# A hybrid layer on one Trainium2 core: stick-breaking v as a fifth seven-product pair, a longer weave, and T1 sums by accumulating loads

## The chip, the core and the metric

The kernel runs on one core of one Trainium2 chip. The core has TensorE (PE, matrix multiplication, 128 x 128), VectorE (DVE), ScalarE (ACT), GpSimd (POOL) and SyncE (SP), a working memory of 128 partitions (SBUF) and eight banks of accumulator memory (PSUM, 512 float32 per partition in each). Every engine takes its instructions in the order in which they were issued to it; SP and POOL also issue DMAs, which all run on the core's 16 DMA engines. The metric is device time in microseconds for one execution, the median of several runs.

## The reference

One layer over 256 tokens of width 2048, all in float32: an FFN (SwiGLU, width 5632), a mixer with two parallel branches, a second FFN, a small embedding gate, with a layer norm after each of the first three. The change concerns the mixer:

```python
proj = x @ w_in
mq, mk, mv, mo, mi, mf, sq, sk, sv, ga, gb = _split_cols(proj)
qk = jax.nn.silu(_causal_conv(jnp.concatenate([mq, mk], axis=-1), conv_w))
...
h = _mlstm_chunkwise(q, k, mv, log_i, log_f)          # 4 heads of 256
h = _head_norm(h, norm_g)
y_m = h * jax.nn.sigmoid(mo)
y_sb = _stick_breaking(sq, sk, sv)                    # 8 heads of 128
merged = jax.nn.sigmoid(ga) * (y_m @ w_up_m) + jax.nn.sigmoid(gb) * (y_sb @ w_up_sb)
return merged @ w_out
```

`w_in` has 11272 columns: q, k, v and output gate of the mLSTM (1024 each), eight gate columns, stick-breaking q, k and v (1024 each), and the two branch gates ga and gb (2048 each).

## The kernel before

**Weights and units.** A weight tile is 256 rows by 512 columns of a weight matrix (512 KB). It is loaded into a page ("raw", one of 48 pages of 4 KB per partition), and then split into two float32r parts: ScalarE casts the high part (line 1213), VectorE subtracts to get the low part (line 1217). A *unit* of the program is six matmuls (lines 1264 to 1266, twice): one weight tile against one token tile of 128, high by high, high by low and low by high. A plain *group* of 512 output columns has eight weight tiles, each used by two units (both token tiles), so 16 units.

**Pairs of seven products.** `seven` and `both7` compute two column groups at once with seven products in the manner of Strassen-Winograd, where the two token tiles and the two groups are the halves. For each of the four chunks of 512 rows there are the products 1 and 2 (of plain weights), and 5, 7, 6, 4, 3, whose weights are sums of raw tiles and whose activations are sums too ("forms", made by `form_turn`). A pair has 28 units, each with a weight of its own, so 28 splits. Product 1 and 2 go first; the five others are interleaved chunk by chunk, so that five PSUM banks are held until the last chunk. The first sum, T1, is b11 + b12. With `loaded` false VectorE makes it (`plus`, line 361); with `loaded` true the raw tile b12 is loaded, and b11 is added by an accumulating DMA from GpSimd's queue (line 1190), and in the last chunk the third sum is made so too. The FFNs' pairs are loaded.

**Order.** A planner walks the program unit by unit and issues the instructions of all engines in the final order. It keeps a clock of its own (`sched.now`, 6 x 0.2161 for a unit) and a heap of small tasks with due times (`DELAY`), which it runs after each unit; `bank` and `spaced` push tasks that need a PSUM bank at least `BANK_GAP` apart. Splits are issued until the number in hand reaches a limit, and raw tiles are loaded up to a limit as well (`HELD`: raw tiles and splits for each mode, set by `Mode` marks in the program). All PSUM tiles, products and small ones alike, share eight banks.

**The mixer.** Its program is, in this order: six plain groups (q of heads 0 and 1; the gates with stick-breaking q of heads 0 and 1; the other q and k groups), then the mLSTM tasks are spawned, then two groups for the mLSTM's v; then the forms of x1T are spawned (`forms_later`); then two plain groups, stick-breaking v of heads 0 to 3 and k and q of heads 0, 1, 2, 3; then `sticks` spawns the eight heads of stick-breaking; and then the *weave*. `weave(main, side)` deals the units of the side list evenly between the units of the main list. Main has 144 units: stick-breaking projections (the second half of v among them), the two gates of column group 0 (`branch`), and the up-projections of groups 0, 1, 2 (`ups`). Side has four pairs, 112 units: the mLSTM's output gate, and the pairs of gates of column groups 1, 2 and 3. After the weave come the up-projections of group 3 and the output projection.

**Tasks.** `mlstm(h)` goes through five PSUM tiles: the decay matrix (line 857), scores (867), numerator with denominator for each token tile (881). VectorE reads the denominator from PSUM three times in small operations (882 to 885), and ScalarE then scales the numerator out of PSUM. `gated(h)` waits for the output gate, multiplies, transposes into PSUM (916) and splits the result into ymT, which is put away to DRAM by `put_ym_away` and brought back by `bring_ym_back`, before the up-projections use it. `stick(h)` needs q, k and v of its head (lines 935 to 965); heads start `STICK_GAP` apart.

Each column of the window tables below is one engine; the DMA share is that of the 16 DMA engines.

Of the kernel before, what the change touches and what calls it, by code (L numbers as in the profile page):

```python
# [13 lines left out]
P = 128  # L14
# [15 lines left out]
HELD = {"ffn": (8, 6), "mix": (5, 6), "wide": (8, 6)}  # L30
# [16 lines left out]
STICK_GAP = 14.0  # L47
# [138 lines left out]
def kernel(  # L186
# [30 lines left out]
    def bank(delay):  # L217
        return sched.slot(delay, BANK_GAP)
# [469 lines left out]
    def sb_columns(ps, t, heads):  # L688

        n = len(heads) * DS  # L690
        if heads[0] >= 16:
            if ("sv", t) not in st:
                st["sv", t] = big()
            c0 = (heads[0] - 16) * DS
            nc.scalar.copy(st["sv", t][:, c0:c0 + n], ps[:, :n])
            flags.update(("sv", t, h - 16) for h in heads)
        else:
            stage = temp()
            nc.scalar.copy(stage[:, :n], ps[:, :n])
            sched.spaced(sb_turn(t, stage, heads), DELAY["sbt"], BANK_GAP)  # L700
# [152 lines left out]
    def mlstm(h):  # L853
        yield from wait("gates", ("qk", 0, h), ("qk", 1, h), ("v", 0, h // 2), ("v", 1, h // 2))
        d = temp()
# [5 lines left out]
        yield DELAY["m0"]  # L861
# [9 lines left out]
        yield DELAY["m1"]  # L871
        mv = small.tile([P, TT, 2], F32, name="hmv", tag="hmv")
        r = small.tile([P, TT], F32, name="hr", tag="hr")
        if ("hs", h // 2) not in st:
            st["hs", h // 2] = big().rearrange("q (g t e) -> q g t e", g=2, t=TT)
        hs = st["hs", h // 2][:, h % 2]
        for t in range(TT):
            ps = misc([P, DM + 1])
            for s in range(t + 1):
                off = s * 256 + (t - s) * P  # L880
                nc.tensor.matmul(ps[:], d[:, off:off + P], st["v", s, h // 2][:, h % 2], start=(s == 0), stop=(s == t))  # L881
            nc.vector.tensor_scalar(out=r[:, t:t + 1], in0=ps[:, DM:], scalar1=-1.0, scalar2=st["em"][:, t, h:h + 1],
                                    op0=ALU.mult, op1=ALU.max)
            nc.vector.tensor_tensor(out=r[:, t:t + 1], in0=ps[:, DM:], in1=r[:, t:t + 1], op=ALU.max)
            nc.vector.reciprocal(out=r[:, t:t + 1], in_=r[:, t:t + 1])
            yield DELAY["m2"]
            activate(hs[:, t], ps[:, 0:DM], ACT.Copy, scale=r[:, t:t + 1])
# [15 lines left out]
    def gated(h):  # L903
# [6 lines left out]
        for t in range(TT):  # L910
            nc.vector.tensor_tensor(out=hs[:, t], in0=hs[:, t], in1=st["mo", t][:, h * DM:(h + 1) * DM], op=ALU.mult)
        for t in range(TT):
            yield bank(0.0 if t else DELAY["m4"])
            ps = misc([P, 2, P])
            for b in range(2):
                nc.tensor.transpose(ps[:, b], hs[:, t, b * P:(b + 1) * P], ident[:])
            dst = ymT.get(h // 2, t)
            parts = [(dst[:, :, 2 * (h % 2) + b], ps[:, b], st["cw"][:, 64 + 2 * h + b:65 + 2 * h + b]) for b in range(2)]
            for d, src, g in parts:
                activate(d[:, 0], src, ACT.Copy, scale=g)  # L920
            for d, src, g in parts:
                nc.vector.scalar_tensor_tensor(out=d[:, 1], in0=src, scalar=g, in1=d[:, 0], op0=ALU.mult, op1=ALU.subtract)
# [54 lines left out]
    for which, g in ((0, 1), (1, 0), (1, 1)):  # L977
        program.extend(flat(group(w_in, range(0, D, 2 * P), which * 1024 + g * COL, COL, x1T, qk_done(which, g))))
    program.append(lambda: [sched.spawn(in_sequence([mlstm(a), mlstm(a + 1)])) for a in (0, 2)])
    for g in range(2):  # L980
        program.extend(flat(group(w_in, range(0, D, 2 * P), 2048 + g * COL, COL, x1T, v_done(g))))
    program.append(lambda: [sched.spawn(forms_later(x1T, c), 6.0 + 14.0 * c) for c in range(4)])

    def sb(*heads):
        if heads[0] >= 16:
            col0 = sq0 + heads[0] * DS
        else:
            col0 = [(sq0 + h * DS, 2 * DS) for h in heads[::2]]
# [3 lines left out]
    program.extend(sb(16, 17, 18, 19))  # L992
    program.extend(sb(8, 9, 2, 3))
# [308 lines left out]
```

## Time and profile before

| | us |
|---|---|
| median of 3 runs | 2188.23 |
| lowest, highest | 2187.34, 2188.68 |
| the profiled execution, its own time | 2186.12 |
| its span (first to last instruction) | 2184.4 |
| end of the mLSTM's v groups, in the span | 855.38 |
| start of the weave | 908.72 |
| start of the last up-projections | 1272.77 |

The profile is of one execution. Its page has the busy time of each engine, the DMA queues, the chain of work that ended last, and groups of instructions by line; further views of the same trace give the busy time in any window, the waits, and the instructions in order of time. A row of a group reads: line, engine, operation, output<-inputs, shapes, count | busy us, mean ns of one | idle time just before them and who ended it. A row of the timeline reads: start, length, engine, line, operation. q1 is the hardware queue that SP feeds, q0 the software queue that GpSimd feeds. Granted TensorE clock was 1.00 in the whole span.

### The profile page before, as it was taken

The page shows a single profiled execution, that of the slowest core. Times are in us where ns is not written, and L with a number is a line of the kernel's source. Part 1 is how long each engine was busy: PE and PEld are TensorE (multiplying, and loading weights), DVE is VectorE, ACT ScalarE, POOL GpSimd, SP SyncE. Part 2 cuts the span into 40 slices and gives each one's busy share as a digit, 9 for nine tenths or more (in the row PEclk, how much of TensorE's full clock was granted, in tenths as well). Part 3 has the DMA queues.
Part 4 walks back from the last instruction along what each step waited for, and adds up shares of the span by engine and source line. Part 5 has one row for each costly group of instructions (what it writes and reads, how often), then busy time and mean ns, then how long its engine had stood idle before and what let it go on. Part 6 is the DMA issues. An engine that isn't in the chain of part 4 may idle for free.

```text
span 2184.4 us, 28262 instructions
## 1 busy us (share of the span) xinstructions
PE 2174.9 (100%) x9966; PEld 1800.5 (82%) x9966; DVE 1903.3 (87%) x2108; ACT 1316.2 (60%) x1591; POOL 97.9 (4%) x88
## 2 busy tenths in 40 slices
PE   9999999999999999999999999999999999999999
PEld 7888888888888888888888888888888888888888
DVE  6899999999998865898988985799999999999974
ACT  7565655556664754667775554566665556665572
POOL 0100000010000000000000000000010000000000
PEclk9999999999999999999999999999999999999999
DMA  9899999999994775667878886589999999999753
GB/s 332 252 302 284 289 293 308 281 277 315 310 331 158 219 229 154 193 210 207 301 216 282 268 270 212 181 237 310 286 278 305 297 283 291 312 299 316 254 165 103
DMA packets 302223, 568.52 MB, mean 260 GB/s; under 512 B 18265, under 2 KB 39681, under 8 KB 302081
## 3 DMA queue, kind: packets, MB, share of 16 engines
q1 hardware_dynamic: 280320, 524.77, 72.0%
q0 software_dynamic: 21760, 41.95, 11.2%
q8 instruction: 78, 1.28, 0.2%
q14 instruction: 65, 0.52, 0.1%
HBM read 560.35 MB, written 6.29 MB: 259 GB/s over the span
## 4 chain that ended last, share of the span: by engine, by line
PE 98%; DVE 1%; ACT 0%; issue 0%; DMA 0%; SPq 0%; DVEq 0%; ACTq 0%
PE mm L1264 31%; PE mm L1266 31%; PE mm L1265 31%; PE ms L290 1%; DVE split L1217 1%; PE ms L495 0%; ACT split L1213 0%; PE ms L959 0%; PE ms L867 0%; PE ms L881 0%; PE ms L935 0%; PE ms L948 0%; DMA big<-in_x_dram 0%; PE ms L705 0%; DVE raw L361 0%
## 5 line engine op out<-in xcount | busy, mean ns | idle before, releaser
L1213 ACT CAST split<-raw 128x1024 fp32r<-128x1024 f32 (+2 forms) x1061 | 1060.7, 1037 | 514.2 <-PE mm L1265 144.4
L1217 DVE TENSOR_TENSOR split<-raw,split 128x1024 fp32r<-128x1024 f32 (+2 forms) x1061 | 1242.9, 1203 | 129.8 <-ACT split L1213 113.9
L1264 PE MATMUL mm<-split,actT 128*128 128x512 f32 (+2 forms) x3120 | 1216.7, 390 | 0.1
L1266 PE MATMUL mm<-split,actT 128*128 128x512 f32 (+2 forms) x3120 | 1203.0, 386 | 1.7 <-DVE actT L297 1.7
L1265 PE MATMUL mm<-split,actT 128*128 128x512 f32 (+2 forms) x3120 | 1201.7, 385 | 0.0
L1266 PEld LDWEIGHTS mm<-split,actT 128*128 128x128 f32 x3120 | 586.0, 188 | 122.7 <-DVE actT L297 3.4
L1265 PEld LDWEIGHTS mm<-split,actT 128*128 128x128 f32 x3120 | 586.9, 188 | 114.1 <-DVE split L1217 2.0
L1264 PEld LDWEIGHTS mm<-split,actT 128*128 128x128 f32 x3120 | 586.6, 188 | 114.3 <-issue 1.3
L361 DVE TENSOR_TENSOR raw<-raw 128x1024 f32<-128x1024 f32 x240 | 293.0, 1221 | 2.2
L1190 POOL DMA_DIRECT2D raw<-in_ffn_w_dram x80 | 95.4, 1193 | 1877.5 <-DVE temp L559 774.1
L292 ACT CAST actT<-ms 128x512 fp32r<-128x512 f32 x60 | 35.1, 587 | 86.5 <-PE ms L290 84.7
L568 DVE TENSOR_TENSOR temp<-mm,temp 128x512 f32<-128x512 f32 x112 | 77.0, 687 | 3.5 <-PE mm L1266 1.3
L621 DVE SCALAR_TENSOR_TENSOR big<-mm,big 128x512 f32<-128x512 f32 x96 | 65.6, 685 | 4.8 <-PE mm L1266 4.8
L297 DVE TENSOR_TENSOR actT<-ms,actT 128x512 fp32r<-128x512 f32 x60 | 40.9, 687 | 19.4 <-ACT big L296 10.6
L236 ACT ACT_TABLE_LOAD x35 | 44.9, 1283 | 0.6
L285 DVE TENSOR_TENSOR actT<-temp,actT 128x512 fp32r<-128x512 f32 x40 | 26.5, 689 | 17.3 <-ACT actT L284 17.2
L240 ACT ACTIVATE temp<-mm 128x512 f32<-128x512 f32 (+1 forms) x22 | 12.2, 559 | 43.6 <-PE mm L1266 43.5
L240 ACT ACTIVATE temp<-temp 128x512 f32<-128x512 f32 (+1 forms) x48 | 28.6, 595 | 9.2 <-DVE temp L568 6.6
L284 ACT CAST actT<-temp 128x512 fp32r<-128x512 f32 x40 | 24.1, 620 | 13.1 <-DVE temp L308 12.2
L794 DVE SCALAR_TENSOR_TENSOR temp<-ms,cw,temp 128x253 f32<-128x253 f32 (+2 forms) x48 | 22.4, 480 | 7.3 <-ACT temp L240 6.1
L1076 DVE SCALAR_TENSOR_TENSOR big<-big,mm 128x512 f32<-128x512 f32 x8 | 5.5, 686 | 25.3 <-PE mm L1266 25.3
L240 ACT ACTIVATE temp<-ms,gbT 128x128 f32<-128x128 f32 x64 | 24.1, 460 | 5.5 <-PE ms L495 5.5
(128 smaller groups left out, 539.5 us busy)
## 6 DMA issues: line engine op xcount, KB each, us to landing
raw<-in_ffn_w_dram SPq DMA_DIRECT2D x655, 512.0 KB, 6.2
raw<-in_w_in_dram SPq DMA_DIRECT2D x176, 512.0 KB, 4.4
raw<-in_ffn_w_dram POOLq DMA_DIRECT2D x80, 512.0 KB, 8.9
raw<-in_w_out_dram SPq DMA_DIRECT2D x32, 512.0 KB, 6.4
raw<-in_w_in_dram SPq DMA_DIRECT2D x56, 256.0 KB, 3.6
raw<-in_w_ple_gate_dram SPq DMA_DIRECT2D x24, 512.0 KB, 6.0
raw<-in_w_up_sb_dram SPq DMA_DIRECT2D x16, 512.0 KB, 5.1
raw<-in_w_up_m_dram SPq DMA_DIRECT2D x16, 512.0 KB, 5.5
```

Source lines behind the costliest of these rows:

```text
L236: nc.scalar.preload_act_table_set(table[0])
L240: nc.scalar.activation(out, in_, func, **kw)
L297: nc.vector.tensor_tensor(out=dst[:, 1], in0=ps[:], in1=dst[:, 0], op=ALU.subtract)
L361: nc.vector.tensor_tensor(out=out.tile[:, :, :cols], in0=a.tile[:, :, :cols], in1=b.tile[:, :, :cols], op=ALU.add)
L568: nc.vector.tensor_tensor(out=out, in0=a, in1=b, op=op)
L621: nc.vector.scalar_tensor_tensor(out=xs, in0=ps, scalar=0.5, in1=xs, op0=ALU.mult, op1=ALU.add)
L1190: nc.gpsimd.dma_start(out=r.tile[:, :, :r.cols], in_=r.plus[0], accum_op=ALU.add)
L1213: nc.scalar.copy(hi[:, ks], r[:, ks])
L1217: nc.vector.tensor_tensor(out=lo[:, ks], in0=r[:, ks], in1=hi[:, ks], op=ALU.subtract)
L1264: nc.tensor.matmul(ps, hi, w[0][:, k, :u.cols], start=first, stop=False)
L1265: nc.tensor.matmul(ps, hi, w[1][:, k, :u.cols], start=False, stop=False)
L1266: nc.tensor.matmul(ps, lo, w[0][:, k, :u.cols], start=False, stop=last)
```

## The change

- Stick-breaking v (1024 columns) leaves the main list and the plain groups, and becomes a fifth pair of seven products, first in the side list, with T1 made by VectorE. `sv_dest` and `sv_ready` place its four results and set the flags for which the sticks wait.
- The weave begins where the two plain groups were: main still has 144 units (the k and q group of heads 0, 1, 2, 3 is now its first), side has 140. In its first part a new mode, "woven", holds six raw tiles instead of eight; the mode "wide" begins after two main groups.
- The four other pairs are made with `loaded` true.
- The forms of x1T are spawned after the second group of mLSTM q, 16 instead of 14 apart.
- `mlstm` asks for its PSUM tiles through `bank`. ScalarE copies numerator and denominator out of PSUM for each token tile, VectorE works on the denominators of both tiles from SBUF (four small operations a head instead of six), and ScalarE scales in SBUF.
- `gated` transposes both token tiles into one PSUM bank.
- `bring_ym_back` is issued half a group earlier, and the up-projections of group 0 use ymT first instead of ysbT. `STICK_GAP` is 13 instead of 14.

```diff
-HELD = {"ffn": (8, 6), "mix": (5, 6), "wide": (8, 6)}
+HELD = {"ffn": (8, 6), "mix": (5, 6), "woven": (6, 6), "wide": (8, 6)}
...
-STICK_GAP = 14.0
+STICK_GAP = 13.0
...
+    def sv_dest(k, t):
+        if ("sv", t) not in st:
+            st["sv", t] = big()
+        return st["sv", t][:, k * COL:(k + 1) * COL]
+
+    def sv_ready(k, t):
+        flags.update(("sv", t, 4 * k + h) for h in range(4))
...
     def mlstm(h):
         yield from wait("gates", ("qk", 0, h), ("qk", 1, h), ("v", 0, h // 2), ("v", 1, h // 2))
+        yield bank(0.0)
...
-        yield DELAY["m0"]
+        yield bank(DELAY["m0"])
...
-        yield DELAY["m1"]
+        yield bank(DELAY["m1"])
...
-            nc.vector.tensor_scalar(out=r[:, t:t + 1], in0=ps[:, DM:], scalar1=-1.0, scalar2=st["em"][:, t, h:h + 1],
-                                    op0=ALU.mult, op1=ALU.max)
-            nc.vector.tensor_tensor(out=r[:, t:t + 1], in0=ps[:, DM:], in1=r[:, t:t + 1], op=ALU.max)
-            nc.vector.reciprocal(out=r[:, t:t + 1], in_=r[:, t:t + 1])
-            yield DELAY["m2"]
-            activate(hs[:, t], ps[:, 0:DM], ACT.Copy, scale=r[:, t:t + 1])
+            nc.scalar.copy(hs[:, t], ps[:, 0:DM])
+            nc.scalar.copy(den[:, t:t + 1], ps[:, DM:])
+            yield DELAY["m2"] if t else bank(DELAY["m2"])
+        nc.vector.tensor_scalar(out=r[:], in0=den[:], scalar1=-1.0, scalar2=None, op0=ALU.mult)
+        nc.vector.tensor_tensor(out=r[:], in0=den[:], in1=r[:], op=ALU.max)
+        nc.vector.tensor_tensor(out=r[:], in0=r[:], in1=st["em"][:, :, h], op=ALU.max)
+        nc.vector.reciprocal(out=r[:], in_=r[:])
+        yield DELAY["m2"]
+        for t in range(TT):
+            activate(hs[:, t], hs[:, t], ACT.Copy, scale=r[:, t:t + 1])
+        yield DELAY["m2"]
...
+        yield bank(DELAY["m4"])
+        ps = misc([P, TT, 2, P])
+        parts = []
         for t in range(TT):
-            yield bank(0.0 if t else DELAY["m4"])
-            ps = misc([P, 2, P])
...
+        if which == 0:
+            program.append(lambda: [sched.spawn(forms_later(x1T, c), 6.0 + 16.0 * c) for c in range(4)])
     program.append(lambda: [sched.spawn(in_sequence([mlstm(a), mlstm(a + 1)])) for a in (0, 2)])
     for g in range(2):
         program.extend(flat(group(w_in, range(0, D, 2 * P), 2048 + g * COL, COL, x1T, v_done(g))))
-    program.append(lambda: [sched.spawn(forms_later(x1T, c), 6.0 + 14.0 * c) for c in range(4)])
...
-    program.extend(sb(16, 17, 18, 19))
-    program.extend(sb(8, 9, 2, 3))
...
     def pair(g):
-        return both7(w_in, ga0 + g * COL, ga0 + D + g * COL, x1T, gate_dest(g), gate_ready(g), False)
+        return both7(w_in, ga0 + g * COL, ga0 + D + g * COL, x1T, gate_dest(g), gate_ready(g), True)

     program.append(sticks)
-    main = sb(10, 11, 4, 5) + sb(20, 21, 22, 23) + sb(12, 13, 6, 7) + sb(14, 15) + branch(0, 0) + branch(0, 1) + [bring_ym_back] + ups(0, True) + ups(1) + ups(2)
-    mode("wide")
-    program.extend(weave(main, both7(w_in, 3072, 3072 + COL, x1T, mo_dest, mo_ready, False) + pair(1) + pair(2) + pair(3)))
+    gate = branch(0, 1)
+    main = sb(8, 9, 2, 3) + sb(10, 11, 4, 5) + [Mode("wide")] + sb(12, 13, 6, 7) + sb(14, 15) + branch(0, 0) + gate[:8] + [bring_ym_back] + gate[8:] + ups(0) + ups(1) + ups(2)
+    mode("woven")
+    program.extend(weave(main, both7(w_in, sq0 + 2 * HS * DS, sq0 + 2 * HS * DS + COL, x1T, sv_dest, sv_ready, False)
+                         + both7(w_in, 3072, 3072 + COL, x1T, mo_dest, mo_ready, True) + pair(1) + pair(2) + pair(3)))
```

34 lines of the change are left out of this document (13 added, 21 removed).

## The prediction

> **What bounds the kernel now.** I read the page first, then the chain of waits, then single stretches of the timeline and of the windows.
>
> ```profile
> span 2184.4 us, 28262 instructions
> ...
> PE 2174.9 (100%) x9966; PEld 1800.5 (82%) x9966; DVE 1903.3 (87%) x2108; ACT 1316.2 (60%) x1591; POOL 97.9 (4%) x88
> ...
> PE 98%; DVE 1%; ACT 0%; issue 0%; DMA 0%; SPq 0%; DVEq 0%; ACTq 0%
> ```
>
> The chain that ends last is TensorE almost everywhere. A change is worth what it takes from, or adds to, TensorE's own stream, plus the holes in that stream. The price of a matmul is the distance between starts, not its printed length, since matmuls are pipelined:
>
> ```profile
> 837.69 0.40 PE L1264 MATMUL mm<-split,actT 128*128 128x512 f32 x1
> ...
> 842.26 0.39 PE L1266 MATMUL mm<-split,actT 128*128 128x512 f32 x1
> ```
>
> These are the first and the last of 21 matmuls with nothing between, so one costs (842.26 - 837.69) / 20 = 0.2285 us. In the undisturbed rows further down (1080.62, 1080.85, 1081.08, 1081.31, 1081.53) it is 0.2275; I use 0.2275. A unit (six matmuls) is 1.365 us.
>
> By counting units from the start of the program (496 in the first FFN, then 112 up to the end of the second mLSTM-v group), the weave of before runs from 908.72 to 1272.77 and the two plain groups ahead of it (stick-breaking v, first half, and heads 8, 9, 2, 3) from 855.38 to 908.72. The windows of these, and of a stretch inside the first FFN for comparison:
>
> ```profile
> 855.38:908.72 53.34, 53.34 (x240) 43.59 (x239) 39.96 (x83) 28.63 (x41) 0.00 (x0) 1.00 0.60 178
> 908.72:1010.00 101.28, 101.20 (x462) 83.23 (x461) 90.42 (x105) 74.94 (x102) 0.00 (x0) 1.00 0.71 214
> 908.72:1272.77 364.05, 362.64 (x1677) 300.00 (x1676) 334.84 (x374) 249.90 (x322) 0.00 (x0) 1.00 0.77 244
> 855.38:1272.77 417.39, 415.98 (x1915) 343.59 (x1915) 374.80 (x456) 278.53 (x363) 0.00 (x0) 1.00 0.75 236
> 300.00:600.00 300.00, 299.96 (x1345) 247.99 (x1344) 281.68 (x275) 180.82 (x191) 23.97 (x21) 1.00 0.96 297
> ```
>
> Columns: length; busy PE, PEld, DVE, ACT, POOL; clock; DMA share; GB/s. VectorE is busy 92% of the weave (334.84 / 364.05), DMA 77%. The FFN, which already loads its T1 sums, runs at 94% DVE and 96% DMA with TensorE closed up. The holes in the mixer's TensorE stream, from its timeline:
>
> ```profile
> 1080.62 0.39 PE L1265 MATMUL mm<-split,actT 128*128 128x512 f32 x1
> 1080.85 0.39 PE L1266 MATMUL mm<-split,actT 128*128 128x512 f32 x1
> 1081.08 0.39 PE L1264 MATMUL mm<-split,actT 128*128 128x512 f32 x1
> 1081.31 0.39 PE L1265 MATMUL mm<-split,actT 128*128 128x512 f32 x1
> 1081.53 0.39 PE L1266 MATMUL mm<-split,actT 128*128 128x512 f32 x1
> 1082.61 0.44 PE L705 MATMUL ms<-ident,temp 128*128 128x128 f32 x2 [0.69 <-DVE temp L950]
> ...
> 1063.31 0.39 PE L1266 MATMUL mm<-split,actT 128*128 128x512 f32 x1
> 1064.05 0.92 PE L935 MATMUL ms<-big 128*128 128x256 f32 x4 [0.36 <-DVE actT L922]
> ...
> 1141.16 0.39 PE L1266 MATMUL mm<-split,actT 128*128 128x512 f32 x1
> 1141.78 0.89 PE L959 MATMUL ms<-temp,big 128*128 128x256 f32 x4 [0.23 <-DVE temp L950]
> ```
>
> Start to start, less one matmul: 0.85, 0.51 and 0.39, 1.75 us together. Each is a small matmul that waits until VectorE has read an old PSUM bank. What VectorE was doing ahead of the first of them stands in the chain:
>
> ```profile
> 1076.54 3.49 DVE split L1217 x3
> 1080.03 0.48 DVE temp L944
> 1080.87 1.22 DVE split L1217
> 1082.09 0.47 DVE temp L950
> 1082.61 0.44 PE ms L705 x2
> ```
>
> The reader that frees the bank (L950) stood behind four splits. So the mixer has two kinds of time to win: matmuls, and under 2 us of holes made by a late VectorE.
>
> **The change part by part.** *Matmuls.* Stick-breaking v was two plain groups: 2 x 8 weight tiles x 2 token tiles x 6 = 192 matmuls of 128x512. As seven products it is 7 x 4 x 6 = 168. 24 x 0.2275 = **5.46 us less**, on the path. All else that TensorE does keeps its count: transposes of gated heads are packed four to a bank instead of two, the mLSTM matmuls are the same.
>
> *VectorE.* Rows of the weave, by form:
>
> ```profile
> L1217 DVE TENSOR_TENSOR split<-raw,split 128x1024 fp32r<-128x1024 f32 x175 | 209.9, 1221 | 25.7 <-ACT split L1213 22.9 <-PE mm L1265 2.3
> L361 DVE TENSOR_TENSOR raw<-raw 128x1024 f32<-128x1024 f32 x64 | 78.1, 1220 | 0.3
> L396 DVE TENSOR_TENSOR big<-mm,big 128x512 f32<-128x512 f32 x23 | 15.8, 686 | 0.1
> L311 DVE TENSOR_TENSOR temp<-big,temp 128x256 f32<-128x256 f32 x2 | 0.8, 418 | 0.0
> ```
>
> Splits: 28 weights instead of 16, +12 x 1.221 = 14.7. Adds that make weights: the new pair does 16 on VectorE (+19.5); each of the other four pairs drops five (four T1, one T3), -20 x 1.220 = -24.4. Evictions: seven at 0.686 where ScalarE made four copies, +4.8. Sum +14.6. The forms of x1T (per chunk four operations of 0.686 and four of 0.418, 4.4 us, 17.7 in all) leave this stretch: they are now spread over 16 us steps from the second q/k group on. From the end of the v groups to the last up-projection VectorE has then 374.8 + 14.6 - 17.7 = 371.7 us in 417.4 - 5.5 = 411.9, 90%, as before (374.8 / 417.4), and below the FFN's 94%. On average it costs nothing, hidden beside TensorE.
>
> *The new pair's own part* is the tightest. The weave now places 140 side units over 144 main ones, so v's 28 end after 57 units, 77.8 us, plus the mLSTM's matmuls of three heads, each by the chain
>
> ```profile
> 829.56 0.62 PE ms L857 x2
> 835.85 1.31 PE ms L867 x8
> 842.65 0.43 PE ms L881 x2
> 845.80 0.87 PE ms L881 x4
> ```
>
> 3.23 us, together 87.5. Its last 20 side units carry all the adds and evictions: with 20.6 main units they last 55.4 us and one head 3.2, 58.6; VectorE needs 20 x 1.221 + 16 x 1.220 + 4.8 + 10.3 x 1.221 = 61.3, and some 3 for a head (an estimate: seven to ten operations between the 0.42 and the 0.69 shown, or shorter): 64.3, so it falls **5.7 us behind**. Cover: six splits stand ready, and the weave uses (140 + 72) / 284 = 0.75 split per unit, so they last 8 units, 10.9 us. The same sum for the first pair of before, also made on VectorE, with 25.7 main units: 64.4 us of splits, adds and evictions in 62.4, sticks and the last forms on top, and window 908.72:1010.00 shows TensorE at 101.20 of 101.28. So I take 0.5 us of new holes; bounds 0 (as there) and 5.7 (no cover, since raw tiles are held at 6 there instead of 8).
>
> *mLSTM.* Where ScalarE now copies the numerator and denominator out, VectorE's three reads of PSUM go:
>
> ```profile
>   DVE hr L882: 11.1, 7
> ```
>
> That row (who waited for L881) is VectorE standing still 11.1 us in seven waits, with splits queued behind it. It was harmless in 855.38:908.72, where VectorE had 13 us free, and would not be inside the weave. Taking it away is what lets the mLSTM move; it gains nothing on the path by itself. Cost on ScalarE: 16 more small operations, and 12 more casts, in an engine that is 69% busy in the weave (249.90 / 364.05): nothing.
>
> *T1 by loads.* 20 accumulating loads go to POOL's queue (five a pair, 512 KB), and v reads 24 raw tiles instead of 16. Prices, first from the FFN stretch 300 to 600, then from 855.38 to 1272.77:
>
> ```profile
> q1 hardware_dynamic: 40677, 78.42, 76.1%
> q0 software_dynamic: 5440, 10.49, 20.0%
> ...
> raw<-in_ffn_w_dram POOLq DMA_DIRECT2D x21, 512.0 KB, 8.2
> ```
> ```profile
> q1 hardware_dynamic: 55958, 98.04, 74.8%
> ...
> raw<-in_w_in_dram SPq DMA_DIRECT2D x120, 512.0 KB, 4.3
> ```
>
> An accumulating 512 KB (20 of them, 10.49 MB) takes 0.200 x 300 / 20 = 3.00 us of all 16 engines, twice a plain FFN load (0.761 x 300 / 149.6 = 1.53). In the mixer a plain one takes 0.748 x 417.39 / 98.04 x 0.524 = 1.67, so the accumulating one lies between 3.00 and 3.28. New sum: 312.2 + 8 x 1.67 + 20 x (3.00 to 3.28) = 386 to 391 us in 411.9, **94 to 95%**. Without v's part (24 + 14 loads, 63.5 us in 87.5) there remain 322 to 328 in 324.4: 99 to 101%, against 96% over 300 us of the FFN. So DMA runs at its limit for 320 us. The lead that hides this: eight raw tiles (8 x 1.67 = 13.4) and the six splits (10.9), 24 us; an excess of 1% is 3 us, and if 0.96 is the most that holds, 328 / 0.96 - 324.4 = 17. I cost it at nothing; without the lead it is 17 us.
>
> The Trainium skill (DMA: Bandwidth & Descriptors, Anatomy of one DMA) fits a GpSimd-issued DMA as 2.0 us plus bytes over 436e3. That makes 3.2 us until a 512 KB accumulate has landed, where the row says 8.2, and by its variable part (1.2 us each) DMA would end near 85% and have no part in the result. The trace disagrees, and I go by the rows.
>
> *Holes taken back.* The adds that stood ahead of the bank's readers fall from 64 to 60 in all, but from 16 to 11 in every pair after the first, and the sticks begin under loaded pairs. Of 1.75 us I take half, 0.9; bounds 0 and 1.75. STICK_GAP 13, the earlier return of ymT (half a gate group sooner, so ahead of the up-projection that now reads it first) and its bank spacing change no count.
>
> **Sum:** 2186.12 (the profiled execution) - 5.46 - 0.9 + 0.5 = 2180.3. The median of the runs is 2188.23, 2.1 above it, so 2182.4.
>
> **Rivals.** *The v pair stalls.* VectorE's 5.7 us come through, or ScalarE's casts stand behind adds with banks held: five product banks, two of the main group, one left of eight. For it: the rows of 1081.53. Against: the first pair of before. Price 2 to 5.7: around 2186.
>
> *DMA becomes the bound* in the gate and up-projection part of the weave. Mechanism: raw pages are given back only as TensorE finishes, so the lead is not there when wanted. For it:
>
> ```profile
> SPq L1185 <- PE mm L1266: 234.6, 108, 6.5
> ```
>
> SP waits 234.6 us in the old weave for pages that TensorE still held. Against: the FFN does the same at 96%. Price up to 17 us, 12 in the middle: 2194, slower. It decides from the point where the share stays at 0.96 and splits wait for raws.
>
> *The mLSTM blocks the last bank.* Five PSUM turns a head, three heads in the weave, 15 turns at 0.39 to 0.85: 6 to 13 us, 2191. Against: the first 8 of v's units hold only three banks, and two of the three heads fall there.
>
> *Only the products count:* no hole goes, none comes: 2182.8; this I hold within the forecast.
>
> **How the numbers follow.** Forecast (2180 to 2184) 0.55; v pair 0.20; DMA 0.15; mLSTM 0.10. A measurement of this kernel tells 0.2%, 4.4 us, from no change: faster is below 2183.9, slower above 2192.6. Faster: 0.52 + 0.05 from a mild v stall = 0.57. Within: 0.03 + 0.14 + 0.04 + 0.03 = 0.24. Slower: 0.01 + 0.11 + 0.07 = 0.19. The range reaches from all holes gone (2188.23 - 5.46 - 1.75, and the 0.9 by which runs lie below their median: 2180; 2179 with the profile's own scatter) to 2193, which leaves out most of the DMA rival's upper half. The forecast's own range is 2180 to 2184.
>
> **What would show it.** Right: 9942 matmuls instead of 9966, the weave's rows 0.2275 apart, no hole over 0.5 us, 20 more issues on POOL, DMA 0.93 or more in the weave, DVE near 90%. Wrong: TensorE gaps before a matmul that ends a chain raw - POOL accumulate - split (DMA), or of L857 to L881 behind DVE or ACT (mLSTM), or gaps between v's units with DVE at 1.0. A shift of time in the FFNs, which are untouched, would make the forecast meaningless.

## The result and the profile after

| | before | after |
|---|---|---|
| median | 2187.94 us (22 runs) | 2191.65 us (22 runs) |
| lowest to highest | 2185.18 to 2189.67 | 2188.90 to 2194.60 |
| profiled execution, its span | 2184.4 | 2188.5 |
| ratio after to before | | 1.0018, 95% interval 1.0011 to 1.0024 |

The changed kernel is slower by 0.18%, 3.7 us. The forecast was 2182.4, faster.

Stage by stage (first matmul of one stage to first matmul of the next, in the two profiles) everything but the weave stayed: start to the end of the v groups 855.38 and 854.90, up-projection 3 with the output projection 113.90 and 113.91, second FFN 691.3 and 691.8, the tail 106.5 and 106.5. The weave's stretch, from the end of the v groups to the last up-projections, took **421.39 instead of 417.39**: 4.0 us more, where 5.5 to 6 less were forecast. The windows of the changed kernel (columns as before), the whole stretch and then parts of it:

```profile
854.90:1276.29 421.39, 414.64 (x1892) 341.64 (x1891) 372.21 (x431) 285.12 (x376) 23.83 (x20) 0.99 0.89 270
...
905.00:955.00 50.00, 50.00 (x228) 41.48 (x227) 46.48 (x56) 34.38 (x48) 1.19 (x1) 1.00 0.86 265
1005.00:1055.00 50.00, 49.93 (x270) 42.42 (x269) 44.33 (x56) 40.01 (x58) 2.39 (x2) 1.00 0.95 292
1055.00:1105.00 50.00, 46.18 (x201) 37.13 (x200) 42.74 (x58) 35.40 (x55) 3.58 (x3) 0.93 0.84 252
1105.00:1155.00 50.00, 50.00 (x225) 41.26 (x224) 42.99 (x49) 34.39 (x43) 3.57 (x3) 1.00 0.96 304
1155.00:1205.00 50.00, 47.25 (x202) 38.50 (x201) 43.67 (x47) 29.09 (x32) 2.38 (x2) 0.97 0.92 279
```

TensorE is closed up everywhere except in two of these windows, and in the same two the granted clock is below 1.00. VectorE (372.21 us) is as busy as worked out, so the loss is no amount of work. To see what it is, take every distance between the starts of two matmuls in the stretch, and subtract the steady one for that shape (0.2275 us for 128x512). What is taken as steady for the small matmuls moves a few us between the first column and the rest, alike in both kernels; it does not move the two columns between them:

| us in the stretch | steady distances | holes over 0.5 | distances 0.15 to 0.24 too long | rest | sum |
|---|---|---|---|---|---|
| before | 413.5 | 1.4 | 1.4 | 1.1 | 417.4 |
| after | 408.0 | 7.3 | 4.1 | 1.9 | 421.4 |

The steady part is a count of matmuls times fixed distances, so it falls by the 24 matmuls, 5.46 us. Three holes ate that, with a slow clock behind them. The timeline of TensorE in the changed kernel:

```profile
1056.38 0.40 PE L1274 MATMUL mm<-split,actT 128*128 128x512 f32 x1
1058.80 0.50 PE L1272 MATMUL mm<-split,actT 128*128 128x512 f32 x1 [2.02 <-DVE actT L931]
...
1060.72 0.63 PE L1274 MATMUL mm<-split,actT 128*128 128x512 f32 x1
1063.15 1.09 PE L925 MATMUL ms<-ident,big 128*128 128x128 f32 x4 [1.80 <-DVE actT L975]
...
1164.92 0.39 PE L1274 MATMUL mm<-split,actT 128*128 128x512 f32 x1
1168.06 0.47 PE L1272 MATMUL mm<-split,actT 128*128 128x512 f32 x1 [2.75 <-DVE big L1025]
```

Start to start less one matmul: 2.19, 2.20 and 2.91 us. By counting units, the matmul at 1058.80 is the first of product 3 of a gate pair, the fifth bank of that pair; the one at 1168.06 is the first of a new main group. Both need a bank, and there is none: five (or four) products, two of the main group, and one or two small tiles hold all eight. The wait at 1063.15 is a small tile waiting for another one. The readers that free the banks are VectorE's (L931 the gated head's low part, L975 a stick's low part, L1025 the product with the gate), and they are late. VectorE at the last hole:

```profile
1159.95 1.23 DVE L1225 TENSOR_TENSOR split<-raw,split 128x1024 fp32r<-128x1024 f32 x1 [0.30 <-ACT split L1221]
1161.09 0.42 DVE L834 TENSOR_TENSOR temp<-temp,bound 128x256 f32<-128x256 f32 x1
1161.43 1.22 DVE L361 TENSOR_TENSOR raw<-raw 128x1024 f32<-128x1024 f32 x1
1162.56 2.35 DVE L1225 TENSOR_TENSOR split<-raw,split 128x1024 fp32r<-128x1024 f32 x2
1164.95 1.23 DVE L361 TENSOR_TENSOR raw<-raw 128x1024 f32<-128x1024 f32 x1
1166.09 1.22 DVE L1225 TENSOR_TENSOR split<-raw,split 128x1024 fp32r<-128x1024 f32 x1
1167.23 0.69 DVE L1025 TENSOR_TENSOR big<-mm,big 128x512 f32<-128x512 f32 x1
1167.83 0.48 DVE L975 TENSOR_TENSOR actT<-ms,actT 128x128 fp32r<-128x128 f32 x2
```

The two readers that free a bank each (L1025, and L975 with its pair) stand behind three splits and two adds for later weights. TensorE had finished the stick's matmuls (L969) at 1162.54 and stood from 1165.31.

### The profile page after: what moved, and what is told of

Read it like the earlier page. It is cut to its first block, busy times and chain, and to the rows that moved or that the text cites. A ratio compares the mean times of both kernels' runs of the same rounds, so it can differ in the third digit from the quotient of the medians.

```text
span 2188.5 us, 28352 instructions
## 1 busy us (share of the span) xinstructions
PE 2173.1 (99%) x9942; PEld 1797.9 (82%) x9942; DVE 1917.3 (88%) x2115; ACT 1327.1 (61%) x1616; POOL 121.7 (6%) x108
## 4 chain that ended last, share of the span: by engine, by line
PE 97%; DVE 1%; DMA 1%; issue 1%; ACT 0%; SPq 0%; DVEq 0%; ACTq 0%
PE mm L1272 31%; PE mm L1274 31%; PE mm L1273 31%; PE ms L290 1%; DMA raw<-in_w_in_dram 1%; DVE split L1225 1%; PE ms L495 0%; PE ms L945 0%; PE ms L869 0%; PE ms L884 0%; DVE raw L361 0%; PE ms L958 0%; PE ms L969 0%; ACT split L1221 0%; DMA big<-in_x_dram 0%
## 5 line engine op out<-in xcount | busy, mean ns | idle before, releaser
L1221 ACT CAST split<-raw 128x1024 fp32r<-128x1024 f32 (+2 forms) x1073 | 1072.5, 1037 | 528.0 <-PE mm L1273 147.8
L1225 DVE TENSOR_TENSOR split<-raw,split 128x1024 fp32r<-128x1024 f32 (+2 forms) x1073 | 1256.3, 1201 | 139.6 <-ACT split L1221 115.6
L361 DVE TENSOR_TENSOR raw<-raw 128x1024 f32<-128x1024 f32 x236 | 287.7, 1219 | 2.4
L1198 POOL DMA_DIRECT2D raw<-in_w_in_dram x20 | 23.8, 1192 | 566.2 <-DVE split L1225 348.0
```

What stands on the lines that cost most here:

```text
L361: nc.vector.tensor_tensor(out=out.tile[:, :, :cols], in0=a.tile[:, :, :cols], in1=b.tile[:, :, :cols], op=ALU.add)
L1198: nc.gpsimd.dma_start(out=r.tile[:, :, :r.cols], in_=r.plus[0], accum_op=ALU.add)
L1221: nc.scalar.copy(hi[:, ks], r[:, ks])
L1225: nc.vector.tensor_tensor(out=lo[:, ks], in0=r[:, ks], in1=hi[:, ks], op=ALU.subtract)
```

## The experiments

Three theories stood at the start: L, the accumulating loads fill the DMA engines; V, VectorE is short in the longer weave whatever the loads do; and the rivals that one rebuilt task (mLSTM, gated) is to blame. Later ones are named in the expectations. "Stretch" and "holes" are those of the tables above, from the one profiled execution of each kernel.

| run | edit | median, us | less before's | ratio to before, 95% | stretch | holes |
|---|---|---|---|---|---|---|
| (changed) |  | 2191.65 | +3.7 | 1.0018 (1.0011 to 1.0024) | 421.4 | 7.3 |
| a1_adds | no accumulating loads | 2195.38 | +8.0 | 1.0033 (1.0022 to 1.0044) | 424.2 | 10.4 |
| a2_old_mlstm | mLSTM body of before | 2192.26 | +4.9 | 1.0020 (1.0012 to 1.0029) | 421.2 | 9.4 |
| a3_old_gated | gated of before | 2194.46 | +7.1 | 1.0030 (1.0020 to 1.0040) | 422.7 | 10.1 |
| b1_loads | before, with the loads | 2188.46 | +1.1 | 1.0003 (0.9994 to 1.0012) | 416.8 | 1.1 |
| c1_gated5 | GATED_GAP 5 | 2193.02 | +6.0 | 1.0032 (1.0020 to 1.0045) | 423.4 | 8.8 |
| c2_bank45 | BANK_GAP 4.5 | 2197.20 | +10.2 | 1.0047 (1.0034 to 1.0059) | 424.0 | 12.4 |
| c3_split5 | five splits ahead | 2190.11 | +3.1 | 1.0013 (1.0005 to 1.0022) | 417.7 | 5.2 |
| c4_gated5_stick | GATED_GAP 5, shorter sticks | 2191.95 | +5.0 | 1.0023 (1.0013 to 1.0033) | 421.1 | 8.2 |
| d2_no_bank | gated without a bank | 2190.75 | +3.5 | 1.0014 (1.0006 to 1.0023) | 418.5 | 7.8 |
| e1_split5_stick | five splits, shorter sticks | 2192.74 | +5.5 | 1.0029 (1.0019 to 1.0039) | 423.6 | 7.5 |
| e2_weight | five splits, weave by columns | 2187.18 | -0.1 | 0.9998 (0.9989 to 1.0007) | 417.9 | 6.5 |
| b2_split5 | before, five splits ahead | 2186.46 | -0.8 | 0.9997 (0.9988 to 1.0006) | 416.5 | 1.2 |
| f1_no_fifth | without the fifth pair | 2194.44 | +7.6 | 1.0034 (1.0021 to 1.0047) | 423.1 | 5.8 |
| e7_weight6 | weave by columns | 2185.61 | -1.3 | 0.9995 (0.9986 to 1.0003) | 415.2 | 4.5 |
| e5_balanced | weave by VectorE's cost, five splits | 2201.23 | +14.4 | 1.0058 (1.0043 to 1.0073) | 419.7 | 5.4 |
| e6_balanced6 | the same, six splits | 2199.53 | +12.7 | 1.0059 (1.0047 to 1.0071) | 418.6 | 7.0 |
| e9_readers | readers of small banks on ScalarE | 2186.91 | -0.3 | 0.9996 (0.9988 to 1.0005) | 416.7 | 4.4 |
| e8_weight_readers | e7 and e9 together | 2187.01 | -0.2 | 0.9993 (0.9984 to 1.0002) | 412.8 | 2.2 |

The kernel before ran beside each group of runs, with medians from 2186.87 to 2187.94; differences between runs below are those of the fourth column. The stretch is of a single execution: in the kernels whose edits lie in the weave alone, the part ahead of it took 854.8 to 858.1 us. So the medians decide, and the stretches only show where the time went.

**The loads are not to blame.** a1 sets `loaded` to False for the four pairs, b1 sets it to True in the kernel before:

```diff
-        return both7(w_in, ga0 + g * COL, ga0 + D + g * COL, x1T, gate_dest(g), gate_ready(g), True)
+        return both7(w_in, ga0 + g * COL, ga0 + D + g * COL, x1T, gate_dest(g), gate_ready(g), False)
...
-                         + both7(w_in, 3072, 3072 + COL, x1T, mo_dest, mo_ready, True) + pair(1) + pair(2) + pair(3)))
+                         + both7(w_in, 3072, 3072 + COL, x1T, mo_dest, mo_ready, False) + pair(1) + pair(2) + pair(3)))
```

> The changed kernel with all five pairs made by VectorE (no accumulating loads). Theory L (the loads fill the DMA engines, raw tiles and with them splits come late, VectorE's evictions are late, TensorE gets holes of over 2 us and then a slower clock): the two groups of holes near 1056 and 1165 go, DMA share in the weave falls to about 0.80, time 2183 to 2186. Theory V (VectorE is short of time in the longer weave whatever the loads do): 20 more adds, 24 us of VectorE, make it worse, 2194 or more.

> The kernel before with only the loads: its four pairs in the weave get T1 (and the last third sum) by accumulating loads. Theory L: DMA share in the weave rises from 0.77 to about 0.94, holes appear, 2190 or more. Theory V: 24 us less on VectorE close the holes of before, 2186 to 2188.

Without loads the changed kernel loses another 4.3 us, and its three waits stand where they stood, the one for L975 0.9 us longer, with three smaller holes of 0.8 us beside them. The waits of TensorE in the stretch (for whom, us in total, times, longest), of a1:

```profile
PE mm L1272 <- DVE big L1025: 2.7, 1, 2.7
PE ms L925 <- DVE actT L975: 2.7, 1, 2.7
PE mm L1272 <- DVE actT L931: 2.0, 1, 2.0
```

The kernel before with loads stays as it was. Theory L falls; of V it fits that VectorE's 24 us matter in the new weave, and not in the old one.

**The rebuilt tasks are not to blame either.** a2 and a3 put back the bodies of `mlstm` and of `gated`:

> The changed kernel with the mLSTM body of before (VectorE reads the denominators in PSUM, no bank spacing). Theories L and V: holes near 1056 and 1165 lie after the mLSTM and stay; 2191 within 1.5, or up to 2 more for VectorE's waits of 11 us inside the weave. Theory M (the new mLSTM body itself shifts ScalarE's and VectorE's order and costs the time): 2188 or less.

> The changed kernel with the gated task of before (one token tile per bank, two transposes each). Theory G (a bank that is held for four ScalarE and four VectorE operations is the one for which TensorE waits at 1056.38, and the wait at 1060.72 follows): both holes go, 4.4 us and 1.8 us of slow clock, 2185 to 2187. Theory L: 2190 to 2192, holes of similar size at another bank.

a2 is 1.2 us behind the changed kernel, with the same three waits and one of 1.2 us inside the mLSTM (L882). a3 is 3.4 us worse, with a hole of 5.2 us at a stick's matmul that waits for a gated head's bank: by these runs, packing four transposes into one bank was a gain of the change.

**Moving the small tiles in the plan.** If a hole needs a small tile in the wrong unit, other gaps should move it. The edits are of constants: `GATED_GAP` 10 to 5 (c1); `BANK_GAP` 3.0 to 4.5 (c2); with c1's also `s0` 7 to 6, `s1` 9 to 7, `s3` 5 to 4, `s4` 6 to 5 (c4); and `"wide": (8, 6)` to `(8, 5)` (c3).

> The changed kernel with GATED_GAP 5 instead of 10. In program order the gated heads' banks then come at weave units 125, 130, 137, 142 (125, 135, 139, 148 before this edit), a stick's bank at 139; the fifth product of the pair starts at unit 138, the next main group with eight banks wanted at 206, a stick's last bank at 205. Theory P (TensorE waits because a small tile holds the eighth bank exactly where a fifth product or a new main group starts): a bank at 137 and one at 205 still stand in the way, holes of 2 to 5 us stay near both places, 2190 to 2193. Theory D (gated heads and sticks together overload VectorE): the burst is denser, the holes grow, 2193 or more.

> The changed kernel with BANK_GAP 4.5 instead of 3. No small bank is asked for between units 130 and 139, but two sticks' banks at 203 and 207, around the main group that starts at 206. Theory P: the holes at the fifth product (unit 138) go, 4 to 6 us with the slow clock behind them; the hole at 206 stays; 2185 to 2188. Theory D: the amount of work is the same, 2190 to 2193.

> The changed kernel with five splits instead of six ahead in the mode wide. Theory Q (the readers that free banks stand behind up to six splits in VectorE's queue): the holes shrink by about a sixth of their wait, 2189 to 2191. Rival: the lead of the splits is what is short, and with less of it the holes grow, 2193 or more.

> The changed kernel with GATED_GAP 5 and shorter planned steps of a stick (s0 6, s1 7, s3 4, s4 5 instead of 7, 9, 5, 6). The last stick's bank comes at unit 189 instead of 204, far ahead of the main group at 206; near the fifth product at 138 there are sticks at 133 and 135 and no gated head between 128 and 140. Theory P: the hole at 206 goes, the one at 138 shrinks or goes; 2184 to 2187. Theory D: sticks and gated heads are denser, 2191 or more.

c4 took the hole at unit 206 away, as theory P had it: with the last stick's bank at unit 189 instead of 204, no wait over 1 us is left there. But the times did not follow: near the gated heads other waits came, of one bank's reader each time. The longest of c4, then of c2 in its two holes:

```profile
PE ms L925 <- DVE actT L931: 3.9, 1, 3.9
```
```profile
PE ms L945 <- DVE actT L931: 2.9, 1, 2.9
PE mm L1272 <- DVE big L1025: 3.0, 1, 3.0
```

c2, for which P forecast that the hole at 138 goes, was the worst of the four: P by itself does not hold. D misses it too, since 2197.20 lies above its 2190 to 2193. Of c2's other holes, most are waits for splits, 3.5 us in five waits. c1 kept holes near both places (4.4 and 3.4 us) and does not tell P from D. Five splits ahead instead of six helped by 0.6 us, within the intervals; in the profiled execution the holes at 138 and 206 were gone, and the wait for L975 was left. The control b2, the same edit in the kernel before, moved nothing beyond its interval:

> The kernel before with five splits ahead in the mode wide, as a control for the changed kernel with five. Theory Q: its three holes (1.75 us) shrink, 2186 to 2187.5. If five are simply better by 1.5 us everywhere, 2185.5; if it only helps where TensorE waits for a bank for long, no change.

**Bank or backlog.** d2 takes the bank away from the gated heads and leaves their operations on ScalarE and VectorE. It leaves out the transposes of the mLSTM's output, 16 small matmuls, so it no longer computes the layer:

```diff
-        ps = misc([P, TT, 2, P])
...
-                nc.tensor.transpose(ps[:, t, b], hs[:, t, b * P:(b + 1) * P], ident[:])
...
-                parts.append((ymT.get(h // 2, t)[:, :, k], ps[:, t, b], st["cw"][:, 64 + 2 * h + b:65 + 2 * h + b]))
+                parts.append((ymT.get(h // 2, t)[:, :, k], hs[:, t, b * P:(b + 1) * P], st["cw"][:, 64 + 2 * h + b:65 + 2 * h + b]))
```

> The changed kernel in which the four gated heads take their ScalarE and VectorE operations from SBUF (the product before the transposes) instead of from PSUM: the same operations and shapes, but no PSUM bank and no transposes (16 matmuls of 128 less, about 2 us of TensorE). It leaves out the transposes of the mLSTM's output. Theory P (banks): the holes at weave units 138 and 139 (near 1056 and 1060) go, the one at 206 stays; 2191.65 less 4.4, less 1.8 of slow clock, less 2: 2183 to 2186. Theory D (VectorE and ScalarE overloaded there): the operations are still in the queues, holes of a few us stay near 1060 at a stick's bank or at a split; 2188 to 2191.

The waits for L931 are gone, the one at unit 206 stayed, and the next small tile, a stick's scores behind another stick's scan (L958), took the place of the first:

```profile
PE ms L943 <- DVE temp L958: 3.8, 1, 3.8
PE mm L1270 <- DVE big L1023: 2.9, 2, 2.8
```

That is theory D's outcome, and its time lies in D's range. A hole needs two things at once, a late VectorE and a bank whose reader it is; which bank it is changes with the edit.

**Is VectorE late because the weave is too dense?** How far VectorE is ahead can be read from the trace: the first matmul of a weight starts, its split has ended so much sooner. The mean and the least of that lead, in us:

| stretch | before | after | e7_weight6 |
|---|---|---|---|
| v pair's part, 860 to 950 | 10.0, 3.7 | 6.8, 3.9 | 6.6, 4.1 |
| 1015 to 1057 | 5.2, 2.6 | 2.8, 1.0 | 4.2, 2.7 |
| 1060 to 1130 | 4.8, 1.3 | 5.1, 1.9 | 3.8, -0.6 |
| 1130 to 1165 | 5.3, 3.3 | 1.8, 0.4 | 1.8, 0.3 |

The first row of before holds its two plain groups too, where a weight lasts two units; from the start of its weave the mean is 6.9. The two lows of the changed kernel in this table lie just ahead of its holes, as the one low of before (1.3, near 1075) lies at its smaller ones. A low lead alone does not make a hole, though: from 1240 to the end of the stretch the changed kernel's lead is 1.8 on the mean and -0.4 at least, and there is none over 0.5 us. (Below zero: a first matmul needs only the high part.) The narrow group of 256 columns ends just ahead of the first: its units last half as long, and the weave dealt it as many side units as any other. e2 and e7 count a main unit by its columns (e2 with five splits):

```diff
-    n = sum(isinstance(u, Unit) for u in main)
+    n = sum(u.cols / COL for u in main if isinstance(u, Unit))
...
-            seen += 1
+            seen += u.cols / COL
```

> The changed kernel with five splits ahead, and a weave that counts a main unit by its columns, so that the narrow group of 256 columns gets half as many side units per main unit. Theory N (the narrow group is where VectorE falls behind, just ahead of the fifth product at 138, since a side unit with its split of 1.22 us and its adds comes there every 2.0 us instead of every 2.7): the lead of the splits near 1020 to 1050 grows by some 3 us, the hole near 1060 goes; 2184 to 2187. Rival (banks alone): a hole of 2 to 4 us stays near the gated heads, 2189 to 2191.

> The changed kernel with the weave weighted by columns, six splits ahead as changed: sets apart the two edits of the earlier run with five (2187.18). Theory N: the weighting is what matters, 2186 to 2189. Theory Q (the readers stand behind six splits): without the five splits only half of it is left, 2189 to 2191.

e7 is 5.0 us faster than the changed kernel, level with the one before. The lead near 1015 to 1057 grew by 1.4 us, not 3, and the holes of 2.2 us near 1056 and 1061 are gone; two of 1.9 and 1.8 came at 1079 and 1108, both behind L975, a stick's low part. The hole near 1165 is gone as well, although the lead ahead of it is as short as in the changed kernel. e2, with five splits as well, gained 3.8: the weighting made all of it, and Q is a weak part at best. e5 and e6 tried to deal side units by VectorE's cost:

> The changed kernel with five splits ahead and a weave that deals side units by VectorE's cost (a split 1.22 us, an add 1.22, an eviction 0.69, against 0.93 of TensorE's time), up to 8 units ahead of or 5 behind an even deal. Theory N: VectorE's lateness is spread, holes of over 1 us go, 2182 to 2186. Rival (a bank in the wrong place, wherever it falls): holes at other places, 2187 to 2191.

> The same balanced weave with six splits ahead. Theory N: as with five, 2182 to 2186. Theory Q: 1.5 us or more above the run with five.

They say little of the question, because `weave` also deals the FFNs' units: the second FFN alone went from 691.8 to 698.9 us. In the mixer itself holes of 5.4 and 7.0 us stayed, which is no support for N. e1, five splits with shorter sticks, was worse than five splits alone:

> The changed kernel with five splits ahead in the mode wide and the shorter steps of a stick together. If the two holes have two causes that each of these edits treats (five splits: readers of banks stand less far back in VectorE's queue; shorter steps: the last stick's bank at unit 187 instead of 204), 2187 to 2189, no hole near 1165. If it is one shortage that only moves, 2190 or more.

**Without the fifth pair.** Stick-breaking v goes back to two plain groups, now in the weave; the lines that copy its columns out are not shown:

```diff
-    main = sb(8, 9, 2, 3) + sb(10, 11, 4, 5) + [Mode("wide")] + sb(12, 13, 6, 7)
+    main = sb(16, 17, 18, 19) + sb(8, 9, 2, 3) + sb(10, 11, 4, 5) + sb(20, 21, 22, 23) + [Mode("wide")] + sb(12, 13, 6, 7)
...
-    program.extend(weave(main, both7(w_in, sq0 + 2 * HS * DS, sq0 + 2 * HS * DS + COL, x1T, sv_dest, sv_ready, False)
-                         + both7(w_in, 3072, 3072 + COL, x1T, mo_dest, mo_ready, True) + pair(1) + pair(2) + pair(3)))
+    program.extend(weave(main, both7(w_in, 3072, 3072 + COL, x1T, mo_dest, mo_ready, True) + pair(1) + pair(2) + pair(3)))
```

> The changed kernel without the fifth pair: stick-breaking v goes back to two plain groups, now inside the weave's main list (first and fourth group), and the side list has its four pairs; loads, mLSTM, gated heads, gaps and the weave's early begin stay as changed. 24 matmuls more than the changed kernel, 5.46 us. Theory N (five pairs among 144 main units make the weave too dense for VectorE in places): with 112 side units among 176 the holes go: 2185 to 2188, no hole over 1 us in the weave. Rival (the other parts make the holes): holes of 2 us and more stay, 2192 or more.

N missed: two holes of 3.2 and 2.6 us remain. They are not the same ones, though. Both wait for ScalarE, in a kernel whose splits are 4 us and more ahead on the mean in almost every 10 us of the weave:

```profile
PE ms L932 <- ACT temp L240: 3.0, 1, 3.0
PE mm L1278 <- ACT big L240: 2.4, 1, 2.4
```

So density makes VectorE's lateness, but a new order of the weave can put a bank's request ahead of its reader, on ScalarE too. The size counts as well. The changed kernel is 3.7 us slower with 5.46 us of matmuls less, 9.2 us in all; f1, with the matmuls of before, is 7.6 us slower. So, in f1's order of the weave, the other parts of the change make a loss of much the same size without the fifth pair. a1, a2 and a3 clear the loads, the mLSTM body and the gated heads one by one; the weave's earlier begin and order, the shorter `STICK_GAP`, the earlier return of ymT and the earlier forms were not tried apart from each other.

**The readers themselves.** In e9 the bank of a stick's result and of a gated head is emptied by one ScalarE copy; VectorE's operations stay, and read the copy:

```diff
-                parts.append((ymT.get(h // 2, t)[:, :, k], ps[:, t, b], st["cw"][:, 64 + 2 * h + b:65 + 2 * h + b]))
+                parts.append((ymT.get(h // 2, t)[:, :, k], hs[:, t, b * P:(b + 1) * P], st["cw"][:, 64 + 2 * h + b:65 + 2 * h + b]))
+        nc.scalar.copy(hs.rearrange("q t (b s) -> q t b s", b=2), ps[:])
...
-        parts = [(ysbT.get(h // 4, t)[:, :, h % 4], ps[:, t * P:(t + 1) * P]) for t in range(TT)]
+        nc.scalar.copy(z[:, 0:S], ps[:])
+        parts = [(ysbT.get(h // 4, t)[:, :, h % 4], z[:, t * P:(t + 1) * P]) for t in range(TT)]
```

> The changed kernel, in which the bank of a stick's result and of a gated head is emptied by one ScalarE copy into SBUF (into tiles that are dead by then), and the further ScalarE and VectorE operations read the copy. VectorE has the same operations, ScalarE 8 copies of 256 and 4 of 512 columns more. Theory R (TensorE waits because these banks' readers stand in VectorE's late queue): the waits for L931 and L975 (2.0 and 1.8 us) go, and the wait at weave unit 206 goes or shrinks, since the last stick's bank is free sooner; with the slow clock behind them 6 to 10 us, 2182 to 2186. Theory D (VectorE itself is late, and some other bank takes their place): holes of 2 us and more stay, 2188 to 2192.

> The same, with the weave weighted by columns (six splits ahead). The earlier weighted run (2185.61) had two holes left, 1.9 us before L925 and 1.8 us before L945, both waiting for VectorE at L975. Theory R: both go, 2181 to 2184, faster than the kernel before. Theory D: 2185 to 2188.

e9 is 4.0 us faster than the changed kernel. The waits for L931 and L1025 are gone, and the one for a stick's bank is 1.1 us; the longest that is left is for a reader that still is VectorE's (L961, the scan). Its waits:

```profile
PE ms L946 <- DVE temp L961: 2.0, 1, 2.0
PE ms L925 <- ACT actT L975: 1.1, 1, 1.1
PE mm L1275 <- DVE split L1227: 0.8, 1, 0.8
```

VectorE was just as late in e9 (lead from 1130 to 1165 again 1.8 on the mean, 0.4 at least), and the hole at 1165 did not come: it is the reader that counts, not the lateness by itself. The FFN of the kernel before, too, has no hole over 0.5 us from 300 to 600 with a lead of 2.9 on the mean and -0.4 at worst; that its fewer small tiles are why was not tried. e8 has the shortest stretch of all, 412.8 against the 411.9 worked out in the prediction, and its profiled execution took 2182.11. But its eleven runs lie in two bunches, five from 2182.1 to 2183.8 and six from 2187.0 to 2188.4, so no gain over the kernel before is shown. The granted clock was 0.999 or 1.00 in both bunches, so it is not the slow clock. What the slower bunch waits for wasn't profiled.

## Why the prediction was wrong, point by point

- **Matmuls, 5.46 us less:** right: 9942 matmuls instead of 9966, and the distance of 0.2275 us held.
- **VectorE's sum, 371.7 us, 90%:** 372.21 was measured, 88% of the longer stretch. The conclusion drawn from it, "On average it costs nothing, hidden beside TensorE", is the step that failed. The sum is right, but the cost isn't made by the sum: with it, the forecast had new holes in the v pair's part alone, and put the rest of the weave at none. There the runs showed 7.3 us of holes, behind readers that came late in VectorE's queue.
- **The v pair's part as the tightest place:** wrong. TensorE was at 50.00 of 50.00 there (905.00:955.00), and the lead never fell below 3.9 us. The holes came 110 to 220 us later, where gated heads, sticks, the narrow group and the start of a pair's five products meet, and where the first up-projections meet the last stick. The working did not look at these places.
- **The cover of 10.9 us:** wrong too, and part of the same step. It was counted from the planner's limit of six splits and not read from the trace. In the weave of before the splits were some 5 us ahead on the mean and 1.3 at least; in the changed one the mean near the holes was 2.8 and 1.8. And the lead covers only splits: the readers that ended the last hole, at 1167.23 and 1167.83, stood behind the splits and adds that VectorE still had to do.
- **Holes: 0.9 taken back, 0.5 new:** 1.4 became 7.3, and 2.7 us of slow clock came on top, for which the working had no term. The net of -0.4 us became +5.9 of holes. 5.9 + 2.7 + 0.8 in the rest - 5.46 is the 4.0 by which the stretch grew.
- **T1 by loads, nothing:** better than that. An accumulating load took 0.148 x 421.39 / 20 = 3.12 us of the 16 engines, inside the 3.00 to 3.28, and DMA came to 0.89 of the stretch, not 0.94, because a plain load cost less than taken: 0.741 x 421.39 / 102.91 x 0.524 = 1.59 us instead of 1.67. The two rows of the changed kernel's stretch stand below this list. Without the loads VectorE costs 4.3 us (a1).
- **The rivals:** "DMA becomes the bound" falls with a1. "The mLSTM blocks the last bank" falls with a2. "The v pair stalls" had the mechanism, banks whose readers stand behind adds, with the count of eight banks and the rows of 1081.53 as its sign, but at the wrong place and with a price for one pass instead of three holes. Its 2186 was too low as well.

```profile
q1 hardware_dynamic: 58798, 102.91, 74.1%
q0 software_dynamic: 5440, 10.49, 14.8%
```

What is settled: the loss is holes in which TensorE waits for a PSUM bank whose reader is late in its engine's queue, and the slow clock behind them; spreading the side units over the narrow group (e7) or taking the readers off VectorE (e9) brings 5.0 and 4.0 us back. What stays open: which part of the change makes them. No part that was taken back by itself ends the loss, and f1 shows one of much the same size without the fifth pair. All kernels with the old order of the weave (before, b1, b2) have 1.1 to 1.4 us of holes, and all with a new one 2.2 to 12.4, also without the fifth pair (f1).

## What to carry to other kernels

A stage in which every engine but TensorE has 10% or more to spare can still lose what an edit saves, if a resource of eight banks is full: look at each place where a bank is asked for, who reads the bank it needs, and what stands ahead of that reader in its queue. Read the slack of a producer from the trace (its end against its consumer's start), not from the limit that the planner allows. Empty a small PSUM tile with the engine whose queue is short, and do the rest from SBUF.

## What the runs showed of the hardware

After some holes TensorE ran at half its clock for a while. In the 20 traces of this case, the times at which the granted clock changes lie whole multiples of 3.41 us apart: in the changed kernel 1059.26, 1066.09, 1168.49 and 1171.90, which are 6.83, 102.40 and 3.41 us from one to the next. So cut the span into windows of 3.41 us that end at these times. Windows of the changed kernel around its first two holes, around the last one, and then windows of c2 around its hole of 3.03 us (columns as before; the first number behind the length is how long TensorE was busy, the number after POOL's is the clock):

```profile
1055.85:1059.26 3.41, 1.39 (x6) 0.82 (x6) 3.41 (x8) 2.53 (x6) 1.20 (x1) 1.00 0.52 141
1059.26:1062.67 3.41, 2.09 (x6) 1.07 (x4) 3.38 (x6) 0.96 (x1) 0.00 (x0) 0.50 0.98 165
1062.67:1066.09 3.42, 2.94 (x9) 2.57 (x10) 3.42 (x5) 0.71 (x3) 0.00 (x0) 0.50 1.03 352
1066.09:1069.50 3.41, 3.41 (x16) 2.77 (x15) 1.42 (x6) 1.74 (x4) 0.00 (x0) 1.00 0.32 131
```
```profile
1165.08:1168.49 3.41, 0.66 (x4) 0.42 (x3) 3.41 (x6) 1.04 (x1) 0.24 (x1) 1.00 0.95 327
1168.49:1171.90 3.41, 3.41 (x10) 2.66 (x9) 3.41 (x4) 0.00 (x0) 2.15 (x2) 0.50 0.76 151
1171.90:1175.32 3.42, 3.42 (x16) 2.81 (x16) 1.82 (x3) 2.33 (x3) 0.00 (x0) 1.00 1.13 203
```
```profile
1062.52:1065.94 3.42, 1.72 (x8) 1.10 (x6) 3.42 (x5) 2.22 (x6) 0.00 (x0) 1.00 1.01 256
1065.94:1069.35 3.41, 2.24 (x11) 1.93 (x12) 2.29 (x7) 1.13 (x2) 0.00 (x0) 1.00 0.93 296
```

The hole of 2.19 us lies in one window, which leaves TensorE 2.02 us idle, and the next window runs at 0.50; so does the one after the hole of 2.91 us (2.75 us idle). c2's hole of 3.03 us is longer than both, but falls on two windows, 1.70 and 1.17 us idle, and the clock stays at 1.00; its hole of 3.14 us is split in the same way. Over all 20 traces, from 20 to 2170 us, the clock was halved after each of the 19 windows at full clock that were idle for 1.94 us or more, and after one other, in e1, that was idle for 1.53 us; the longest idle time that left it at 1.00 is 1.93 us (f1). The ends of matmuls are modelled in the profile, so the limit is rough. It is the idle time in a window that counts, some 57% of it in these runs, and where a hole falls decides whether it costs more than itself. In the changed kernel the full clock came back after a window that was busy for 2.94 us, and not after the one that was busy for 2.09. The other four runs of c2 took a mean clock of 0.997 to 0.999 where the profiled one had 1.00.

At clock 0.50 the matmuls start 0.425 us apart. The two slow stretches of the changed kernel cost 2.7 us, a third of what the holes themselves did. The Trainium skill (TensorE: Matmul & The Clock Gate, Part 1: The HAM clock gate) says that the clock is halved after an idle window of about 3.4 us, that the window runs freely, and that it takes a busy window to come back. The trace agrees with the half, with the length of the window and with its running freely. But the window need not be idle throughout: here the clock fell after holes of 2.2 to 2.9 us, so a limit of 3.4 us on each hole would not have kept this kernel at full clock.
